# Layer 1's token decays as wide operations, with the weight split moved to ScalarE and VectorE

## The chip, the cores and the metric

The kernel runs on one core of a Trainium2 chip. The metric is the device time of one launch in microseconds (us), the median of repeated runs. A core has five engines that work side by side, each through its own instructions in program order: TensorE (PE in the profile; its weight loads are PEld), VectorE (DVE), ScalarE (ACT), GpSimd (POOL) and SyncE (SP), which here only issues transfers. An engine that waits holds up everything behind it in its own row of instructions. "Sq" behind an engine's name is its queue.

## The reference

One inference step over 128 context and 1024 latent tokens, two layers. Layer 0 mixes with gated linear attention, layer 1 with a gated DeltaNet; each is followed by a gated feed-forward block. The change is in layer 1's preparation, which cut to its core is, per head (8) and direction (2), in chunks:

```
q, k, v = split(silu(dwconv(u @ w_in)))          # width-3 convolution over tokens
qh = l2norm(q) * dk**-0.5 ;  kh = l2norm(k)
g = -exp(a_log) * softplus(a + dt_bias) ;  beta = sigmoid(bt)
b = cumsum(g)                                     # inside a chunk
ld = exp(where(i >= j, b_i - b_j, -inf))
kk  = strict_lower(einsum('id,jd->ij', kh * beta, kh) * ld)
aqk = einsum('id,jd->ij', qh, kh) * ld
t   = inverse(I + kk)
qd = qh * exp(b) ;  kd = kh * exp(b_last - b)
```

A scan over the chunks follows, then the output projection. The kernel works with chunks of 128 tokens (9 of them) and keeps the lengths of q and k apart, to be divided out later.

## The kernel before

**Stage.** `in_proj1` (L1306) multiplies the layer's input (1024 features, 1152 tokens) by 33 weight blocks of 1024x128, in three token chunks of 384. A chunk of a block is 24 matmuls of 384 columns: each f32 product is made of three (L307 to L309), from a rounded high part and a low rest of weight and input. One block makes q, k, v or the gate z of a head; heads get three or four blocks (the last, seven). The product lies in one of seven PSUM tiles ("ps"), and ScalarE copies it out (`evac_raw`, L660, into "rawc"), or applies silu to it for z.

**Weights.** `Weights.fill` (L237) takes a block's weights from "raw" (two buffers, loaded by SyncE) and splits them on GpSimd: L244 makes "whi", L245 "wlo"; four buffers each. A block's split is asked for when the block two before it starts, and the next load is issued right after it.

**Background work.** `mm_block` calls `tick` between its matmuls: generators in the queue `bg` advance by one `yield`, `PACE1` = 4 of them in each chunk, one generator after the other. What a step emits is placed in each engine's row there and then. `conv` (three VectorE steps L1354 to L1358, one for each product copied out) makes q, k and v; then it queues `delta_v` or `delta_a`. A second queue, `side`, holds `solve`, a chain of small VectorE steps (L1564, L1566).

**`delta_a` for one head** (L1445): SyncE broadcasts the cumulated decays b of both directions to all partitions ("bc", one buffer, L1452). After three ticks ScalarE squares q (L1458); TensorE transposes k, ScalarE copies it and squares it, and VectorE sums the squares ("ss"). Then exp(bc) goes into "NA" on ScalarE, and GpSimd multiplies it by q (L1488); SyncE stores it in "pack". For each of 9 chunks and 2 directions, VectorE makes min(bc - b, mask) on 128x128 (L1496), and ScalarE its exponential with a per-token bias (L317, "bc<-bc,lrho"). Three matmuls with a one-column weight add q's squares over the features (L1502); ScalarE copies each row of lengths (L1504) and SyncE stores it in "qqd". Then, one tick each, nine chunks: k^T k and k^T q on TensorE (L1509, L1510), and one VectorE multiply by both decays into "NA" (L1511). Stores to "xd", "Nd" and "pack" close the head.

`delta` (L1806) is the next stage; its `lengths` reads qqd back, transposes it on TensorE and takes 1/length.

Of the kernel before, what the change touches and what calls it, by code (L numbers as in the profile page):

```python
# [37 lines left out]
PACE = 6  # L38
PACE1 = 4
LAGA = 3  # L40
GL, EL, SL, LL, ML, PL = 6, 5, 4, 1, 0, 2
# [178 lines left out]
class Weights:  # L220
# [3 lines left out]
    def __init__(self, K, order):  # L224
# [3 lines left out]
        self.dma = None  # L228

    def load(self, upto):  # L230
        while self.loaded < min(upto, self.n):
            t = self.K.wp.tile([128, 1024], F32, name="raw", tag="raw", bufs=NRAW)
            (self.dma or self.K.nc.sync).dma_start(t, self.K.I["wall"][self.order[self.loaded]])
            self.raw[self.loaded] = t
            self.loaded += 1

    def fill(self, upto):  # L237
        K, nc = self.K, self.K.nc
        while self.next < min(upto, self.n):
            self.load(self.next + 1)  # L240
            raw = self.raw.pop(self.next)
            hi = K.wp.tile([128, 1024], F32R, name="whi", tag="whi", bufs=NB)
            lo = K.wp.tile([128, 1024], F32R, name="wlo", tag="wlo", bufs=NB)
            nc.gpsimd.tensor_scalar(hi, raw, 1.0, 0.0, op0=ALU.mult, op1=ALU.add)  # L244
            nc.gpsimd.tensor_tensor(lo, raw, hi.bitcast(F32), op=ALU.subtract)  # L245
            self.tiles[self.next] = (hi, lo)
            self.next += 1
            self.load(self.next + NRAW - 1)
# [7 lines left out]
class Kern:  # L256
# [1049 lines left out]
    def in_proj1(self, pre, swap):  # L1306
# [43 lines left out]
        def conv(h, part, raw):  # L1350
# [43 lines left out]
    def gates_body(self, p):  # L1394
# [36 lines left out]

        nc.vector.tensor_tensor(self.kdl, ptv, self.b, op=ALU.subtract)
        for d in range(2):
# [11 lines left out]
    def delta_a(self, h, qT, kT, tp):  # L1445
# [16 lines left out]
        ss = tp.tile([128, NT], F32, name="ss", tag="ss", bufs=2)  # L1462
        for n0 in range(0, NT, 3):
# [11 lines left out]
        self.act(kl, ss, AF.Exp, scale=0.5)  # L1475
        for d in range(2):
            c = 8 * d + h
            nc.vector.tensor_tensor(lrho[:, d], self.lbeta[:, :, c], ss, op=ALU.subtract)
            nc.vector.tensor_tensor(rho[:, d], lrho[:, d], self.kdl[:, :, c], op=ALU.add)
        self.act(rho, rho, AF.Exp)  # L1480

        flat = lambda t: t.rearrange("p n i -> p (n i)")
        for d, t in ((0, Nt[1]), (1, At[1])):
            x = flat(t)
            self.act(x, bc[:, d], AF.Exp)
            for a in (0, TC):
                w = TC if a == 0 else TL
                nc.gpsimd.tensor_tensor(x[:, a:a + w], x[:, a:a + w], qT[:, a + (a > 0):a + (a > 0) + w], op=ALU.mult)  # L1488
            nc.sync.dma_start(self.pack[h, d, :, :, 0].rearrange("n p t -> p n t"), t)
        yield  # L1490

        for d in range(2):
            c = 8 * d + h
            for n in range(NT):
                e = bc[:, d, n * 128:n * 128 + 128]
                nc.vector.scalar_tensor_tensor(e, e, self.b[:, n, c:c + 1], self.v("msk_b" if d else "msk_f"), op0=ALU.subtract, op1=ALU.min)  # L1496
                self.act(e, e, AF.Exp, bias=lrho[:, d, n:n + 1])
                if n % 3 == 2:
                    yield
        for i in range(3):  # L1500
            ps = self.ps()
            nc.tensor.matmul(ps[0:1, :CW], self.v("ones")[:, 0:1], At[0][:, 3 * i:3 * i + 3], start=True, stop=True)  # L1502
            qr = tp.tile([1, CW], F32, name="qr", tag="qr", bufs=2)
            nc.scalar.copy(qr, ps[0:1, :CW])  # L1504
            nc.sync.dma_start(self.qqd[h, i:i + 1], qr)
            yield
        for n in range(NT):
# [298 lines left out]
    def delta(self, up):  # L1806
# [4 lines left out]
        with tc.tile_pool(name="dls", bufs=1, reuse_waits="tile") as tp:  # L1811
# [13 lines left out]

            qq = tp.tile([72, 128], F32, name="qq")
            nc.sync.dma_start(qq, self.qqd.rearrange("h i (n t) -> (h i n) t", t=128))

            def lengths():
                ps = self.ps()  # L1830
                nc.tensor.transpose(ps[:, :72], qq, self.v("ident")[:72, :72])
                rq = self.rq.rearrange("p h n -> p (h n)")
                self.act(rq, ps[:, :72], AF.Sqrt, bias=self.eps)
                nc.vector.reciprocal(rq, rq)
                nc.vector.tensor_scalar(rq, rq, 128.0 ** -0.5, None, op0=ALU.mult)

# [4 lines left out]
            for h in range(8):  # L1841
# [44 lines left out]
    def body(self, es, ew):  # L1886
# [3 lines left out]
        with L("u0", side="right") as up:  # L1890
# [81 lines left out]
```

## Time and profile before

| | us |
|---|---|
| median of 3 runs (lowest to highest) | 3569.97 (3560.07 to 3581.61) |
| the profiled execution, its own time | 3563.03 |
| its span, first to last instruction | 3561.0 |
| TensorE busy | 3194.8 (90%) |
| VectorE busy | 2269.7 (64%) |
| GpSimd busy | 1187.6 (33%) |
| ScalarE busy | 1082.2 (30%) |

The mean clock granted to TensorE is 0.94 of full speed. Layer 1's projection fills about 1606 to 2156 us of the span; a feed-forward stage lies ahead of it, the scan (`delta`) behind it. Busy shares are averages over stages with different limits, so the stage has to be looked at by itself. A row "A <- B" names the wait of A for B.

### The profile page before, as it was taken

To read this page: it belongs to the slowest core of one execution; us is meant where nothing else is said; L and a number is where in the kernel's file an instruction comes from. 1 tells how busy PE (TensorE), PEld (TensorE's weight loads), DVE (VectorE), ACT (ScalarE), POOL (GpSimd) and SP (SyncE) were. 2 spreads that over 40 slices of the span, in tenths; PEclk is the share of its full clock that TensorE was granted. 3 is DMA by queue.
4 is the path that set the end of the run, shared out by engine and by line. 5 is a ranking of instruction groups with operands and counts; after the bars stand their busy time and mean duration, and the time that the engine had idled before them with its cause. 6 is when DMAs were issued, how large, how long until landed. Compare 5 with 4: busy or idle time off the path is not lost.

```text
span 3561.0 us, 54650 instructions
## 1 busy us (share of the span) xinstructions
PE 3194.8 (90%) x21774; PEld 2979.9 (84%) x21774; DVE 2269.7 (64%) x3749; ACT 1082.2 (30%) x2282; POOL 1187.6 (33%) x768
## 2 busy tenths in 40 slices
PE   6988898999999999789879997788869999999887
PEld 4877677899999998778778887688859999999886
DVE  4385565656666677665577784755646676676766
ACT  2434213411111111445353433455553111111133
POOL 1221146222222325543223331344533222322455
PEclk9988979999999999889889998999989999999998
DMA  7312443122222112224554648555401111111132
GB/s 257 99 57 78 162 160 132 66 91 99 89 90 89 42 42 84 83 67 137 154 162 134 216 144 244 167 158 163 126 12 42 42 42 42 43 45 39 60 106 95
DMA packets 248877, 370.18 MB, mean 104 GB/s; under 512 B 67647, under 2 KB 185695, under 8 KB 248240
## 3 DMA queue, kind: packets, MB, share of 16 engines
q1 hardware_dynamic: 240612, 349.54, 30.8%
q10 hardware_dynamic: 7340, 14.92, 1.2%
q8 instruction: 173, 2.83, 0.3%
q0 software_dynamic: 672, 2.23, 0.2%
q14 instruction: 80, 0.66, 0.1%
HBM read 284.69 MB, written 81.93 MB: 103 GB/s over the span
## 4 chain that ended last, share of the span: by engine, by line
PE 64%; DVE 18%; ACT 7%; DMA 7%; issue 2%; SPq 1%; POOL 1%; ACTq 0%; DVEq 0%; POOLq 0%
PE ps L307 18%; PE ps L308 17%; PE ps L309 17%; DVE bc L1496 2%; DVE S L522 2%; DVE lns L531 2%; PE psm L428 1%; DVE lnt L581 1%; DVE cv L737 1%; DVE S L593 1%; ACT UH L621 1%; DMA Nl<-Nd 1%; ACT lnt L623 1%; DVE tY L1564 1%; PE ps L836 1%
## 5 line engine op out<-in xcount | busy, mean ns | idle before, releaser
L307 PE MATMUL ps<-UH,whi 128*128 128x384 f32 (+1 forms) x3408 | 1210.7, 355 | 8.8 <-ACT UH L621 5.3
L308 PE MATMUL ps<-UL,whi 128*128 128x384 f32 (+1 forms) x3408 | 1174.1, 345 | 30.7 <-POOL UL L598 23.2
L309 PE MATMUL ps<-UH,wlo 128*128 128x384 f32 (+1 forms) x3408 | 1170.8, 344 | 3.9 <-POOL wlo L245 3.9
L522 DVE SCALAR_TENSOR_TENSOR S<-ps,mod,S 128x384 f32<-128x384 f32 (+1 forms) x1376 | 603.4, 508 | 457.1 <-PE ps L309 456.2
L244 POOL TENSOR_SCALAR whi<-raw 128x1024 fp32r<-128x1024 f32 x262 | 302.9, 1156 | 1685.8 <-PE ps L308 1178.2
L307 PEld LDWEIGHTS ps<-UH,whi 128*128 128x128 f32 x3408 | 660.0, 194 | 64.7 <-issue 46.0
L308 PEld LDWEIGHTS ps<-UL,whi 128*128 128x128 f32 x3408 | 660.0, 194 | 41.3 <-POOL UL L598 26.2
L245 POOL TENSOR_TENSOR wlo<-raw,whi 128x1024 fp32r<-128x1024 f32 x262 | 662.1, 2527 | 21.8
L309 PEld LDWEIGHTS ps<-UH,wlo 128*128 128x128 f32 x3408 | 659.0, 193 | 4.8 <-POOL wlo L245 4.8
L307 PE MATMUL ps<-hh,whi 128*128 128x384 f32 x1056 | 366.5, 347 | 44.3 <-DVE S L522 20.0
L309 PE MATMUL ps<-hh,wlo 128*128 128x384 f32 x1056 | 362.4, 343 | 4.0 <-POOL wlo L245 4.0
L308 PE MATMUL ps<-hl,whi 128*128 128x384 f32 x1056 | 360.8, 342 | 0.4 <-DVE hl L742 0.4
L317 ACT ACTIVATE cv<-cv 128x1153 f32<-128x1153 f32 (+1 forms) x84 | 82.9, 987 | 769.4 <-DVE cv L696 617.0
L307 PEld LDWEIGHTS ps<-hh,whi 128*128 128x128 f32 x1056 | 202.5, 192 | 56.2 <-issue 29.1
L696 DVE SCALAR_TENSOR_TENSOR cv<-raw,vec,cv 128x1153 f32<-128x1153 f32 x136 | 204.6, 1505 | 4.6
L309 PEld LDWEIGHTS ps<-hh,wlo 128*128 128x128 f32 x1056 | 202.7, 192 | 4.6 <-POOL wlo L245 4.6
L308 PEld LDWEIGHTS ps<-hl,whi 128*128 128x128 f32 x1056 | 202.9, 192 | 1.2 <-DVE hl L742 1.2
L660 ACT COPY raw<-ps 128x384 f32<-128x384 f32 (+2 forms) x272 | 95.1, 408 | 346.1 <-PE ps L309 346.0
L525 POOL TENSOR_TENSOR S<-S,gp 128x384 f32<-128x384 f32 x96 | 97.6, 1019 | 141.5 <-ACT gp L520 141.2
L693 DVE TENSOR_SCALAR cv<-raw,vec 128x1153 f32<-128x1153 f32 x68 | 112.9, 1660 | 13.5 <-ACT raw L660 13.5
L737 DVE SCALAR_TENSOR_TENSOR cv<-ps,vec,cv 128x383 f32<-128x383 f32 (+4 forms) x128 | 61.6, 513 | 81.6 <-ACT edge L733 61.8
L1496 DVE SCALAR_TENSOR_TENSOR bc<-bc,bsum,vecd 128x128 f32<-128x128 f32 x144 | 98.7, 755 | 17.0 <-ACT NA L317 16.9
(291 smaller groups left out, 3996.7 us busy)
## 6 DMA issues: line engine op xcount, KB each, us to landing
raw<-wall SPq DMA_DIRECT2D x260, 512.0 KB
qka<-pack SPq DMA_DIRECT2D x144, 192.0 KB
lnt<-wmod SPq DMA_DIRECT2D x48, 512.0 KB
wm<-wmod SPq DMA_DIRECT2D x40, 512.0 KB
pack<-NA SPq DMA_DIRECT2D x32, 576.0 KB
bc<-brow SPq DMA_DIRECT2D x16, 576.0 KB
Nd<-NA SPq DMA_DIRECT2D x16, 576.0 KB
pack<-cv SPq DMA_DIRECT2D x16, 512.0 KB
```

The costliest lines, as they stand in the source:

```text
L244: nc.gpsimd.tensor_scalar(hi, raw, 1.0, 0.0, op0=ALU.mult, op1=ALU.add)
L245: nc.gpsimd.tensor_tensor(lo, raw, hi.bitcast(F32), op=ALU.subtract)
L307: mm(out, wh, uh, start=first, stop=False)
L308: mm(out, wh, ul, start=False, stop=False)
L309: mm(out, wl, uh, start=False, stop=last)
L522: nc.vector.scalar_tensor_tensor(d, ps[:, lo - c * CW:hi - c * CW], g, d, op0=ALU.mult, op1=ALU.add)
L525: nc.gpsimd.tensor_tensor(d, d, t, op=ALU.add)
L660: nc.scalar.copy(raw[:, d:d + hi - lo], ps[:, lo - c * CW:hi - c * CW])
L693: nc.vector.tensor_scalar(t[i], raws[i][:, 0:n], w[:, 0:1], None, op0=ALU.mult)
L696: nc.vector.scalar_tensor_tensor(t[i], raws[i][:, k:n + k], w[:, k:k + 1], t[i], op0=ALU.mult, op1=ALU.add)
L737: nc.vector.scalar_tensor_tensor(t[i][:, a:b], ps[:, a + o:b + o], w[:, k:k + 1], t[i][:, a:b], op0=ALU.mult, op1=ALU.add)
L1496: nc.vector.scalar_tensor_tensor(e, e, self.b[:, n, c:c + 1], self.v("msk_b" if d else "msk_f"), op0=ALU.subtract, op1=ALU.min)
```

## The change

- **Decays wide.** The 144 steps on 128x128 and their exponentials go. For each direction, `between` adds the bias and takes the minimum with the mask in two VectorE operations on 128x1152 (in place on bc), and one ScalarE exponential on 128x1152 follows. The bias now holds log(beta) - b, made once in the gates.
- **q times its decay** (`decayed`) moves from GpSimd to VectorE; direction 0 goes to At[1], direction 1 to Nt[1]. "rho" becomes a product with a precomputed "wend".
- **Lengths.** Nine matmuls with a one-column moving operand put the lengths into columns of one PSUM tile; one copy writes them to "rq". The store, the load and the transposition of qqd go; the square root stands ahead of the scans.
- **Weights.** In blocks 4 to 32 the split is made by ScalarE (whi) and VectorE (wlo), and it is asked for at the second chunk of a block, one block further ahead.
- **Pace.** Five ticks in a chunk instead of four; each of the nine products takes two ticks; two spare ticks ahead of them; the silu of `conv` gets a step of its own.

```diff
-PACE1 = 4
+PACE1 = 5
...
+LAGN = 2
...
+            if self.shared:
+                nc.scalar.copy(hi, raw)
+                nc.vector.tensor_tensor(lo, raw, hi.bitcast(F32), op=ALU.subtract)
+            else:
+                nc.gpsimd.tensor_scalar(hi, raw, 1.0, 0.0, op0=ALU.mult, op1=ALU.add)
+                nc.gpsimd.tensor_tensor(lo, raw, hi.bitcast(F32), op=ALU.subtract)
...
         def evac(b, c, ps):
...
+            if c == 1 and b > 3:
+                self.W.fill(self.wi + NB - 1)
             self.tick(1, st.get("conv", []))
...
             nc.vector.scalar_tensor_tensor(t, raw[:, 2:1155], w[:, 2:3], t, op0=ALU.mult, op1=ALU.add)
+            yield
             self.silu(t, t)
...
+        def decayed(d, t):
+
+            x = flat(t)
+            self.act(x, bc[:, d], AF.Exp)
+            for a in (0, TC):
+                w = TC if a == 0 else TL
+                nc.vector.tensor_tensor(x[:, a:a + w], x[:, a:a + w], qT[:, a + (a > 0):a + (a > 0) + w], op=ALU.mult)
+            nc.sync.dma_start(self.pack[h, d, :, :, 0].rearrange("n p t -> p n t"), t)
+
+        def between(d):
+
+            e = bc[:, d].rearrange("p (n i) -> p n i", i=128)
+            m = self.v("msk_b" if d else "msk_f").unsqueeze(1).to_broadcast([128, NT, 128])
+            nc.vector.tensor_tensor(e, e, lrho[:, d].unsqueeze(2).to_broadcast([128, NT, 128]), op=ALU.add)
+            nc.vector.tensor_tensor(e, e, m, op=ALU.min)
...
-        for d, t in ((0, Nt[1]), (1, At[1])):
-            x = flat(t)
-            self.act(x, bc[:, d], AF.Exp)
-            for a in (0, TC):
-                w = TC if a == 0 else TL
-                nc.gpsimd.tensor_tensor(x[:, a:a + w], x[:, a:a + w], qT[:, a + (a > 0):a + (a > 0) + w], op=ALU.mult)
-            nc.sync.dma_start(self.pack[h, d, :, :, 0].rearrange("n p t -> p n t"), t)
-        yield
-
-        for d in range(2):
-            c = 8 * d + h
-            for n in range(NT):
-                e = bc[:, d, n * 128:n * 128 + 128]
-                nc.vector.scalar_tensor_tensor(e, e, self.b[:, n, c:c + 1], self.v("msk_b" if d else "msk_f"), op0=ALU.subtract, op1=ALU.min)
-                self.act(e, e, AF.Exp, bias=lrho[:, d, n:n + 1])
-                if n % 3 == 2:
-                    yield
-        for i in range(3):
-            ps = self.ps()
-            nc.tensor.matmul(ps[0:1, :CW], self.v("ones")[:, 0:1], At[0][:, 3 * i:3 * i + 3], start=True, stop=True)
-            qr = tp.tile([1, CW], F32, name="qr", tag="qr", bufs=2)
-            nc.scalar.copy(qr, ps[0:1, :CW])
-            nc.sync.dma_start(self.qqd[h, i:i + 1], qr)
+        decayed(0, At[1])
+        yield
+
+        ps = self.ps()
+        for n in range(NT):
+            nc.tensor.matmul(ps[:, n:n + 1], At[0][:, n], self.v("ones")[:, 0:1], start=True, stop=True)
+        nc.scalar.copy(self.rq[:, h], ps[:, :NT])
+        decayed(1, Nt[1])
+        yield
+        between(0)
+        yield
+        between(1)
+        yield
+        self.act(bc[:, 0], bc[:, 0], AF.Exp)
+        yield
+        self.act(bc[:, 1], bc[:, 1], AF.Exp)
+        for _ in range(LAGN):
             yield
         for n in range(NT):
...
+            yield
             yield
...
         with tc.tile_pool(name="in1", bufs=1, reuse_waits="tile") as p:
             first((2,))
+            self.W.shared = True
             for b in range(4, 33):
                 self.blocks([self.w()], b, range(NC), evac)
+            self.W.shared = False
```

VectorE's row from one head's bias sums to its first products, sixth head; tY and Y are steps of `solve`, "cv" of `conv`. Before:

```order
L1479 TENSOR_TENSOR rho<-lrho,kdl 128x9
L1564 TENSOR_TENSOR tY<-X,Y 128x192
L1566 TENSOR_TENSOR Y<-Y,tY 128x8x24
L1564 TENSOR_TENSOR tY<-X,Y 128x175
L1566 TENSOR_TENSOR Y<-Y,tY 128x7x25
L1496 SCALAR_TENSOR_TENSOR bc<-bc,bsum,vecd 128x128 x12
L1564 TENSOR_TENSOR tY<-X,Y 128x156
L1566 TENSOR_TENSOR Y<-Y,tY 128x6x26
L1564 TENSOR_TENSOR tY<-X,Y 128x135
L1566 TENSOR_TENSOR Y<-Y,tY 128x5x27
L1496 SCALAR_TENSOR_TENSOR bc<-bc,bsum,vecd 128x128 x6
```

And now:

```order
L1480 TENSOR_TENSOR NA<-NA,cv 128x128
L1480 TENSOR_TENSOR NA<-NA,cv 128x1024
L1480 TENSOR_TENSOR NA<-NA,cv 128x128
L1480 TENSOR_TENSOR NA<-NA,cv 128x1024
L1589 TENSOR_TENSOR tY<-X,Y 128x220
L1591 TENSOR_TENSOR Y<-Y,tY 128x10x22
L1589 TENSOR_TENSOR tY<-X,Y 128x207
L1591 TENSOR_TENSOR Y<-Y,tY 128x9x23
L1487 TENSOR_TENSOR bc<-bc,lrho 128x1152
L1488 TENSOR_TENSOR bc<-bc,vecd 128x1152
L1487 TENSOR_TENSOR bc<-bc,lrho 128x1152
L1488 TENSOR_TENSOR bc<-bc,vecd 128x1152
```

Eighteen small steps in two groups have become four wide ones, and the product of q with its decay (L1480), which stood on GpSimd, now lies ahead of them.

ScalarE's row at the same place ("rawc" is a product copied out, "cv" the silu of `conv`). Before:

```order
L317 ACTIVATE NA<-bc 128x1152 x2
L660 COPY rawc_12863<-ps 128x384
L317 ACTIVATE bc<-bc,lrho 128x128 x12
L660 COPY rawc_12863<-ps 128x384
L317 ACTIVATE bc<-bc,lrho 128x128 x6
L1504 COPY qr<-ps 1x384 x2
L660 COPY rawc_12864<-ps 128x128
L660 COPY rawc_12864<-ps 128x256
L1504 COPY qr<-ps 1x384
L660 COPY rawc_12864<-ps 128x384
```

And now:

```order
L324 ACTIVATE NA<-bc 128x1152
L1519 COPY rq<-ps 128x9
L324 ACTIVATE NA<-bc 128x1152
L667 COPY rawc_12862<-ps 128x384
L324 ACTIVATE bc<-bc 128x1152 x2
L667 COPY rawc_12863<-ps 128x128
L667 COPY rawc_12863<-ps 128x256
L248 CAST whi<-raw 128x1024
L667 COPY rawc_12863<-ps 128x384 x2
L322 ACT_TABLE_LOAD
L324 ACTIVATE cv<-cv 128x1153
```

The three copies of lengths (qr), which stood behind the exponentials, have become one (rq) that stands between the first two, and the weights' high part (whi) now stands among the copies out of PSUM.

## Rows read from the trace of the kernel before

**Rows 1.** Windows: a feed-forward stretch and layer 1's projection; columns in the first line.

```profile
core 0: us, PE busy (x) PEld busy (x) DVE busy (x) ACT busy (x) POOL busy (x), PEclk, DMA share, GB/s
700.00:1300.00 600.00, 600.00 (x3613) 568.69 (x3612) 387.85 (x634) 79.15 (x172) 155.35 (x90) 1.00 0.24 81
1640.00:2140.00 500.00, 438.78 (x2440) 405.46 (x2440) 360.34 (x576) 209.73 (x433) 161.75 (x101) 0.92 0.50 157
```

**Rows 2.** The chain of waits by line, 1600 to 2240 us (share of that stretch).

```profile
by line: DVE bc L1496 12.1%; PE ps L307 10.5%; PE ps L308 10.2%; PE ps L309 10.2%; DMA bc<-brow 4.1%; DVE tY L1564 3.2%; PE ps L1509 2.9%; issue 2.8%; PE ps L1510 2.4%; ACT bc L317 1.9%; DVE cv L1358 1.9%; DMA kvd<-vt 1.8%; DMA zd<-zt 1.7%;
```

**Rows 3.** Timeline, TensorE, 1984 to 1996: start us, duration us, instruction, [idle before it].

```profile
1983.75 0.38 PE L1509 MATMUL ps<-cv 128*128 128x128 f32 x2
1983.97 0.39 PE L1510 MATMUL ps<-cv 128*128 128x128 f32 x2
1984.12 0.42 PE L307 MATMUL ps<-UH,whi 128*128 128x384 f32 x1
...
1984.90 0.34 PE L308 MATMUL ps<-UL,whi 128*128 128x384 f32 x1
1985.07 0.34 PE L309 MATMUL ps<-UH,wlo 128*128 128x384 f32 x1
1992.66 0.80 PE L1509 MATMUL ps<-cv 128*128 128x128 f32 x2 [7.25 <-ACT rawc L660]
...
1994.00 0.52 PE L308 MATMUL ps<-UL,whi 128*128 128x384 f32 x1
1994.32 0.52 PE L309 MATMUL ps<-UH,wlo 128*128 128x384 f32 x1
```

**Rows 4.** Timeline, all engines, 1979.5 to 1993, the same columns.

```profile
1980.25 1.17 ACT L317 ACTIVATE NA<-bc 128x1152 f32<-128x1152 f32 x1 [5.39 <-DMA bc<-brow]
...
1981.45 10.18 DVE L1496 SCALAR_TENSOR_TENSOR bc<-bc,bsum,vecd 128x128 f32<-128x128 f32 x12 [5.43 <-ACT NA L317]
...
1981.49 4.93 POOL L1488 TENSOR_TENSOR NA<-NA,cv 128x128 f32<-128x128 f32 x4 [29.62 <-ACT NA L317]
```

**Rows 5.** Timeline, VectorE, 1979.5 to 2000.

```profile
1992.81 1.66 DVE L1496 SCALAR_TENSOR_TENSOR bc<-bc,bsum,vecd 128x128 f32<-128x128 f32 x6
...
1996.38 1.89 DVE L1511 TENSOR_TENSOR NA<-ps,bc 128x512 f32<-128x512 f32 x3
```

**Rows 6.** Waits, 1604 to 2180: who waited for whom, total us, times, longest.

```profile
POOL whi L244 <- DMA raw<-wall: 104.9, 12, 22.0
...
PE ps L1509 <- ACT rawc L660: 27.9, 6, 7.2
...
PE ps L1509 <- DVE NA L1511: 22.4, 4, 10.2
...
ACT NA L317 <- DMA bc<-brow: 16.8, 9, 5.4
...
PE ps L1509 <- ACT qr L1504: 6.8, 2, 4.1
```

**Rows 7.** Groups by line, 1604 to 2180: busy us, mean ns | idle before, releaser.

```profile
L1496 DVE SCALAR_TENSOR_TENSOR bc<-bc,bsum,vecd 128x128 f32<-128x128 f32 x144 | 98.7, 755 | 17.0 <-ACT NA L317 16.9
...
L317 ACT ACTIVATE bc<-bc,lrho 128x128 f32<-128x128 f32 x144 | 47.8, 392 | 49.5 <-DVE bc L1496 49.0
...
L1502 PE MATMUL ps<-NA,vecd 128*1 128x384 f32 x48 | 20.6, 512 | 3.1 <-ACT NA L1467 3.1
...
L317 ACT ACTIVATE NA<-bc 128x1152 f32<-128x1152 f32 x16 | 18.3, 1159 | 16.8 <-DMA bc<-brow 16.8
...
L1459 ACT ACTIVATE NA<-cv 128x1024 f32<-128x1024 f32 x8 | 8.4, 1048 | 0.0
```

**Rows 8.** Groups by line and form, VectorE, 640 to 1600.

```profile
L706 DVE TENSOR_TENSOR hl<-cv,hh 128x1024 fp32r<-128x1024 f32 x18 | 22.0, 1225 | 11.2 <-ACT hh L705 11.2
```

**Rows 9.** Timeline, SyncE's queue, 1970 to 2020.

```profile
2017.51 0.64 SPq L233 DMA_DIRECT2D raw<-wall  x1
```

**Rows 10.** Timeline, GpSimd, 2000 to 2030.

```profile
2025.62 1.06 POOL L244 TENSOR_SCALAR whi<-raw 128x1024 fp32r<-128x1024 f32 x1 [13.36 <-DMA raw<-wall]
```

More of the change, by code (lines that the diff above doesn't have):

```diff
@@ L56 @@
 ILAG = 7
+LAGA = 3
 LAGV = 5
+LAGN = 2
 def _pv(v):
@@ L228, in __init__ @@
         self.dma = None
+        self.shared = False
     def load(self, upto):
@@ L243, in fill @@
             lo = K.wp.tile([128, 1024], F32R, name="wlo", tag="wlo", bufs=NB)
-            nc.gpsimd.tensor_scalar(hi, raw, 1.0, 0.0, op0=ALU.mult, op1=ALU.add)
-            nc.gpsimd.tensor_tensor(lo, raw, hi.bitcast(F32), op=ALU.subtract)
+            if self.shared:
[4 more added lines that the diff above has]
+                nc.gpsimd.tensor_tensor(lo, raw, hi.bitcast(F32), op=ALU.subtract)
             self.tiles[self.next] = (hi, lo)
@@ L1430, in gates_body @@
         self.act(self.dec, ptv, AF.Exp)
-        nc.vector.tensor_tensor(self.kdl, ptv, self.b, op=ALU.subtract)
+        nc.vector.tensor_tensor(self.wend, ptv, self.b, op=ALU.subtract)
+        nc.vector.tensor_tensor(self.wend, self.wend, self.lbeta, op=ALU.add)
+        self.act(self.wend, self.wend, AF.Exp)
+        nc.vector.tensor_tensor(self.lbeta, self.lbeta, self.b, op=ALU.subtract)
         for d in range(2):
@@ L1457, in delta_a @@
         Nt, At = ([NA[:, d, i] for d in range(2)] for i in range(2))
+        flat = lambda t: t.rearrange("p n i -> p (n i)")
+        def decayed(d, t):
[10 more added lines that the diff above has]
+            nc.vector.tensor_tensor(e, e, m, op=ALU.min)
         nc.scalar.activation(At[0][:, 0], qT[:, 0:TC], AF.Square)
@@ L1460, in delta_a @@
         yield
-        ss = tp.tile([128, NT], F32, name="ss", tag="ss", bufs=2)
+        ss = tp.tile([128, 2, NT], F32, name="ss", tag="ss", bufs=2)
         for n0 in range(0, NT, 3):
@@ L1467, in delta_a @@
             nc.scalar.activation(Nt[1][:, n0:n0 + 3].rearrange("p n k -> p (n k)"), ps[:, :CW], AF.Square)
-            nc.vector.tensor_reduce(ss[:, n0:n0 + 3], Nt[1][:, n0:n0 + 3], axis=AX.X, op=ALU.add)
+            nc.vector.tensor_reduce(ss[:, 0, n0:n0 + 3], Nt[1][:, n0:n0 + 3], axis=AX.X, op=ALU.add)
             yield
         nc.sync.dma_start(self.kvd[h, 0], Nt[0])
-        self.act(ss, ss, AF.Ln, bias=self.eps)
         kl, rho = self.kl[:, h], self.rho[:, h]
         lrho = tp.tile([128, 2, NT], F32, name="lrho", tag="lrho", bufs=2)
-        self.act(kl, ss, AF.Exp, scale=0.5)
+        self.act(ss[:, 0], ss[:, 0], AF.Ln, bias=self.eps)
@@ L1476, in delta_a @@
+        self.act(kl, ss[:, 0], AF.Exp, scale=0.5)
+        self.act(ss[:, 1], ss[:, 0], AF.Exp, scale=-1.0)
         for d in range(2):
-            c = 8 * d + h
[L1478 to L1482, printed above, removed]
-        for d, t in ((0, Nt[1]), (1, At[1])):
-            x = flat(t)
-            self.act(x, bc[:, d], AF.Exp)
-            for a in (0, TC):
-                w = TC if a == 0 else TL
-                nc.gpsimd.tensor_tensor(x[:, a:a + w], x[:, a:a + w], qT[:, a + (a > 0):a + (a > 0) + w], op=ALU.mult)
-            nc.sync.dma_start(self.pack[h, d, :, :, 0].rearrange("n p t -> p n t"), t)
@@ L1490, in delta_a @@
-        yield
-        for d in range(2):
-            c = 8 * d + h
-            for n in range(NT):
-                e = bc[:, d, n * 128:n * 128 + 128]
-                nc.vector.scalar_tensor_tensor(e, e, self.b[:, n, c:c + 1], self.v("msk_b" if d else "msk_f"), op0=ALU.subtract, op1=ALU.min)
-                self.act(e, e, AF.Exp, bias=lrho[:, d, n:n + 1])
-                if n % 3 == 2:
-                    yield
-        for i in range(3):
-            ps = self.ps()
-            nc.tensor.matmul(ps[0:1, :CW], self.v("ones")[:, 0:1], At[0][:, 3 * i:3 * i + 3], start=True, stop=True)
-            qr = tp.tile([1, CW], F32, name="qr", tag="qr", bufs=2)
-            nc.scalar.copy(qr, ps[0:1, :CW])
-            nc.sync.dma_start(self.qqd[h, i:i + 1], qr)
+            nc.vector.tensor_tensor(lrho[:, d], self.lbeta[:, :, 8 * d + h], ss[:, 0], op=ALU.subtract)
@@ new lines, in delta_a @@
+            nc.vector.tensor_tensor(rho[:, d], ss[:, 1], self.wend[:, :, 8 * d + h], op=ALU.mult)
+        yield
+        decayed(0, At[1])
[11 more added lines that the diff above has]
+        self.act(bc[:, 0], bc[:, 0], AF.Exp)
@@ L1823, in delta @@
             self.drain([self.inverse(Q[0]["N"], Q[0]["U"], Q[0]["T"], tp)])
[L1826 to L1835, printed above, removed]
+            rq = self.rq.rearrange("p h n -> p (h n)")
+            self.act(rq, rq, AF.Sqrt, bias=self.eps)
+            nc.vector.reciprocal(rq, rq)
+            nc.vector.tensor_scalar(rq, rq, 128.0 ** -0.5, None, op0=ALU.mult)
             def done(h):
@@ L1871, in delta @@
                     nc.sync.dma_start(Q[h]["z"], self.zd[h])
-                if h == 0:
-                    lengths()
                 if h == 3:
@@ L1936, in body @@
             self.load_vec("vecd", p)
-            self.lbeta, self.b, self.kdl = (p.tile([128, NT, 16], F32, name=x) for x in ("lbeta", "bsum", "kdl"))
+            self.lbeta, self.b, self.wend = (p.tile([128, NT, 16], F32, name=x) for x in ("lbeta", "bsum", "wend"))
             self.kl = p.tile([128, 8, NT], F32, name="kl")
```

2 lines of the change are left out of this document (removed).

## The prediction, made before the change was run

> **What bounds the kernel now.** I read the windows first, to see how the stage of the change differs from one that runs well [rows 1]. From 700 to 1300 us TensorE has no gap and a granted clock of 1.00. From 1640 to 2140, in layer 1's projection, it is busy for 438.8 of 500 us, so 61 us are gaps, and the clock is 0.92. The clock has two levels (1.2 and 2.4 GHz), so 0.92 means that 16% of the stretch, 80 us, ran at the low one; work done there takes twice as long, and about 40 us are lost. VectorE is busy for 360 us, ScalarE for 210: neither is full. The stage is TensorE's, less about 100 us that it loses by waiting.
>
> The chain of waits says on whom: the largest single entry, ahead of any matmul line, is VectorE's L1496 with 12.1% [rows 2]. The timeline of TensorE shows one such wait [rows 3]: the matmuls start 0.17 us apart (1984.90, 1985.07), then comes a gap of 7.25 us, until ScalarE has copied a product out of PSUM, and after the gap they start 0.32 us apart, at the low clock. The gap and the clock are one loss with two parts.
>
> Why ScalarE was late stands in the timeline of all engines [rows 4]. The broadcast bc came 5.39 us after ScalarE was ready for it. Then GpSimd multiplied q by its decay for 4.93 us, and in that time and during the weight split behind it twelve steps of L1496 took 10.18 us. A few microseconds later six of them took 1.66 us, 0.277 us each [rows 5]: the steps are short, but not beside GpSimd. ScalarE's exponentials alternate with them, and its copies out of PSUM stand behind those exponentials, so TensorE runs out of its seven PSUM tiles. The first product of the head (L1511) is made at 1996.38, 16.1 us after bc landed. Twelve waits of this kind, on ScalarE's rawc and qr and on VectorE's NA, sum to 27.9 + 22.4 + 6.8 = 57 us [rows 6]; they are nearly all of the 61.
>
> **The change part by part.** The sum is made against the profiled execution, 3563.0 us; the median of the runs is 7 us above it.
>
> VectorE's load. The 144 small steps go: 98.7 us as they stand [rows 7], but only 144 x 0.277 = 40 us if nothing stood beside them; 59 us are contention. In their place come 32 operations on 128x1152. The nearest is the 128x1024 subtraction of the feed-forward, 1.225 us [rows 8], which is itself partly run beside GpSimd; by width that gives 1.38 us, 44 us in all. The product with q comes over from GpSimd: 16 times a 128x1024 (1.2) and a 128x128 (0.25), 23 us. The weights' low part is exactly the operation of rows 8: 29 x 1.2 = 35 us. So VectorE's busy time moves by -99 + 44 + 23 + 35 = +3 us: it stays at about 360 us, 70 to 75% of a shorter stage. The gain isn't in its load, but in where it falls: no burst of 18 steps beside GpSimd, which keeps only the small copies and memsets of `solve`.
>
> ScalarE. 144 exponentials of 0.39 us make room for 16 of 1.16 [rows 7], -38 us; the high part of the weights costs 29 x 1.05 (the 128x1024 square of L1459), +30 us. It stays under half busy.
>
> The chain that TensorE waits for. After bc lands: exponential 1.2, product with q 1.4 for each direction (the second exponential runs beside the first product), four small steps of `solve` 1.5, four wide operations 5.5, the last exponential 1.2: 12.2 us to the first L1511, against 16.1. And three PSUM tiles are no longer held: before, the three copies of lengths stood in ScalarE's row behind all 18 exponentials; now one copy stands ahead of the wide ones. With 2.5 products in a chunk instead of 4, a chunk uses 3.5 PSUM tiles in some 4.9 us (24 matmuls of 0.173 and what lies between them), so three tiles are about 4 us of patience. Against that, TensorE gets to the first product sooner: seven ticks at five a chunk behind the exponential, where it was nine at four, some 4 us. What each head gains by the shorter chain and by the tiles, 8 us, is half eaten by this.
>
> What is late next: the broadcast. It is issued behind the stores of the head before, and ScalarE waited for it nine times, 16.8 us in all, 5.4 at most [rows 6]. The change makes none of these transfers smaller, and a TensorE that waits less gets to that place earlier. I let three or four heads keep a wait of 5 us, and the others 1 us: 22 us of gaps are left of the 61, and clock losses in proportion, 14 of 40. Saved: 39 + 26 = 65 us. Bounds: nothing, if bc stays the end of the chain in every head, and 101, if all waits go.
>
> The lengths. 24 matmuls of 384 columns go, 20.6 us of records [rows 7], on the path wherever TensorE is the end. 72 with one moving column come, but each needs 128 columns of weights. The trace has no such operation. Two matmuls of 128 moving columns with a weight load each take 0.37 us before the next can start (1983.75 to 1984.12) [rows 3], 0.18 each; a single one costs at least nothing and at most the whole pair, 0.37. That is 13 us by the middle value, which I take since it is the nearest row: -7 us net, between -21 and +6. The Trainium skill's "TensorE: Matmul & The Clock Gate", section "LDWEIGHTS (loading the stationary operand)", speaks against this edit: a load costs its columns over 1.2 in ns, whatever the moving side has. By it 144 loads (two passes per matmul, as the 48 records of L1502 for 24 matmuls show) are an estimated 15 us, and the edit would bring 5 us, not 7. No run before has a one-column moving operand.
>
> The new wait. GpSimd waited 12 times for a raw weight, 104.9 us, at most 22.0 [rows 6], and nobody minded, since it runs ahead. Now ScalarE and VectorE wait for it, and behind ScalarE's copy stand the copies out of PSUM. A load issued at 2017.51 [rows 9] was there for GpSimd at 2025.62 [rows 10]: 8 us. In the new order a load is issued when the block before it is split, one block ahead, and a block is at least 72 x 0.173 = 12.5 us of TensorE. That covers 8 us; it doesn't when SyncE is late itself behind a head's stores. I charge 12 us for it and for other queueing in the two rows (below: 0, since seven PSUM tiles hide a wait of a few us; above: the 105 us).
>
> The rest. The readback of the lengths and its transposition leave `delta`; they were a few operations among waits for transfers: nothing. More ticks per chunk and the extra step in `conv` move work by less than a chunk: nothing, unless the stage's end gets a tail.
>
> Sum: 3563.0 - 65 - 7 + 12 = 3503, and 7 more for the median: 3510 us.
>
> **The rivals.** *The broadcast holds.* The chain of stores, load and broadcast of a head is as long as before, TensorE merely gets to it sooner. For it: the waits for bc, and 4.1% of the stage's chain in that transfer [rows 2]. Against it: L1496 has three times that share. Gaps 45, clock 30, lengths -7, new waits 8: -61 + 45 - 40 + 30 - 7 + 8 = -25, 3545 us.
>
> *All waits go.* The pace of one product in two ticks is slow enough for VectorE everywhere: -61 - 40 - 7 and 5 for new waits: -103, 3467 us. Against it: bc's lateness isn't touched.
>
> *Slower: the raw weights stop ScalarE.* If GpSimd's 12 waits fall on ScalarE's row in full, 105 us, and PSUM hides some 4 us of each, 57 us of gaps are new, and by today's ratio of clock to gap (40 to 61) another 37. With 72 saved that is +22: 3592 us. It decides from the point at which a load lands over 4 us behind ScalarE's reaching the copy, in about every third block. For it: the loads stand in SyncE's row among stores that themselves wait for VectorE, which now waits for the loads. Against it: the loads are asked for earlier than before. The same page of the Trainium skill (section "Architectural detail: the array is 16× 32×32, not 1× 128×128") calls the rows of ScalarE and VectorE strictly first in, first out; nothing then gets past such a copy, as the exponentials in rows 4 already show.
>
> *It doesn't do what it says.* If L1496 is slow for another reason than GpSimd, the wide operations would be slow too. The same instruction at 0.277 and at 0.85 us within 12 us speaks against this; its time would be that of the first rival.
>
> **Chances.** The forecast 0.55 (its own range 3485 to 3532), the broadcast holds 0.20, all waits go 0.15, slower 0.10. The range for eight in ten, 3462 to 3562, takes in the first two rivals and leaves the slower one out. What runs of this kernel can tell from no change is about 0.5%, 18 us, so faster means less than 3552 us. That is the forecast, all waits gone and about half of the first rival: 0.81; within 0.5%: 0.10; slower: 0.09.
>
> **What would show it.** Right: in the projection the granted clock rises to 0.96 or more, TensorE's gaps fall to some 20 us, those left stand behind bc or raw; the wide operations take 1.3 to 1.4 us each; the stage is 50 to 70 us shorter, and the stages around it as long as before. The lengths: 72 matmuls in less than 20 us. Wrong: waits of ScalarE for raw of over 40 us in sum, gaps of over 40 us behind it or behind VectorE's wide steps, or wide steps of 2 us and more. A gain that lies outside the stage would be another cause than mine.

## The result, and the profile after

The changed kernel takes 3529.44 us (median of 4 runs, 3509.85 to 3550.28) against 3575.79 for the kernel before (4 runs): a ratio of 0.9886, interval 0.9852 to 0.9919, faster by some 46 us. The forecast was 3510, 60 us below the median of 3 runs known then (3570), with 3462 to 3562 as its range.

To compare profiles I cut out layer 1's projection by its own first and last work, the first copy into `abs` and the last silu into `zt`, and call that the stage. It is a better measure than the whole: the identical code ahead of the stage ended between 1584.9 and 1609.2 us in the 14 profiles of this study, so one run of the whole says little about 20 us, while the stage came out at 531.4 and 528.9 us in two profiles of the changed kernel. The windows of the stage, of the kernel before (columns as in rows 1; the last two lines are a gap and what follows it):

```profile
1588.20:2162.90 574.70, 511.46 (x2844) 475.91 (x2842) 381.42 (x608) 245.41 (x495) 174.77 (x113) 0.93 0.50 159
...
1985.40:1992.60 7.20, 0.01 (x1) 0.00 (x0) 7.10 (x13) 3.31 (x10) 4.43 (x3) 0.84 0.70 217
1992.60:1995.00 2.40, 2.34 (x9) 2.34 (x10) 2.40 (x8) 1.82 (x8) 0.00 (x0) 0.50 0.00 0
```

and of the changed kernel: the two stretches of [rows 1], the stage, and the largest gap that is left with what follows it.

```profile
700.00:1300.00 600.00, 600.00 (x3617) 568.03 (x3616) 386.78 (x628) 80.32 (x175) 155.62 (x90) 1.00 0.23 80
1640.00:2140.00 500.00, 464.00 (x2810) 452.95 (x2810) 336.64 (x553) 204.79 (x336) 17.00 (x19) 0.94 0.55 175
...
1597.50:2128.90 531.40, 499.79 (x2936) 487.00 (x2934) 340.66 (x554) 228.06 (x376) 16.30 (x18) 0.96 0.54 171
...
1973.30:1979.30 6.00, 0.00 (x0) 0.00 (x0) 5.86 (x8) 2.80 (x5) 0.00 (x0) 0.68 0.35 110
1979.30:1982.20 2.90, 2.89 (x10) 2.89 (x11) 2.87 (x6) 1.28 (x2) 0.00 (x0) 0.50 0.00 0
```

The stage is 43.3 us shorter. TensorE's gaps (span less busy) went from 63.2 to 31.6 us; its busy time fell by 11.7. VectorE is busy 40.8 us less, though it took over two kinds of work from GpSimd. The groups by line of the changed kernel, for [rows 7]:

```profile
L249 DVE TENSOR_TENSOR wlo<-raw,whi 128x1024 fp32r<-128x1024 f32 x32 | 39.2, 1224 | 48.5 <-ACT whi L248 43.9 <-issue 4.4
L1366 DVE SCALAR_TENSOR_TENSOR cv<-rawc,vec,cv 128x1153 f32<-128x1153 f32 x24 | 34.4, 1434 | 0.2
...
L1480 DVE TENSOR_TENSOR NA<-NA,cv 128x128 f32<-128x128 f32 (+1 forms) x32 | 22.5, 755 | 15.9 <-ACT NA L324 12.4 <-ACT rq L1519 3.4
L1488 DVE TENSOR_TENSOR bc<-bc,vecd 128x1152 f32<-128x1152 f32 x16 | 21.7, 1358 | 0.6
L1487 DVE TENSOR_TENSOR bc<-bc,lrho 128x1152 f32<-128x1152 f32 x16 | 21.6, 1351 | 0.0
```

And its waits, for [rows 6]:

```profile
ACT bc L324 <- DVE bc L1488: 47.2, 15, 6.6
ACT whi L248 <- DMA raw<-wall: 25.0, 7, 5.0
ACT NA L324 <- DMA bc<-brow: 10.6, 8, 2.9
PE ps L1518 <- ACT NA L1490: 8.1, 2, 5.2
PE ps L1533 <- ACT rawc L667: 6.4, 2, 6.0
PE ps L1533 <- DVE NA L1535: 6.0, 5, 2.7
PE ps L843 <- ACT cv L324: 3.8, 2, 3.2
PE ps L314 <- ACT whi L248: 1.5, 1, 1.5
```

The 57 us that TensorE waited for rawc, qr and NA have become 12.4 (6.4 + 6.0). A new one stands at the lengths, 8.1 us: they now run early, straight behind ScalarE's squares of q (L1490), which wait for the stores of the head before. The largest gap left is the old kind in a new form; here it is in the changed kernel's timeline of all engines:

```profile
1964.90 1.17 ACT L324 ACTIVATE NA<-bc 128x1152 f32<-128x1152 f32 x1 [2.91 <-DMA bc<-brow]
...
1968.08 1.17 ACT L324 ACTIVATE NA<-bc 128x1152 f32<-128x1152 f32 x1 [1.97 <-DMA bc<-brow]
...
1972.16 1.35 DVE L1487 TENSOR_TENSOR bc<-bc,lrho 128x1152 f32<-128x1152 f32 x1
1973.55 1.36 DVE L1488 TENSOR_TENSOR bc<-bc,vecd 128x1152 f32<-128x1152 f32 x1
...
1975.00 1.16 ACT L324 ACTIVATE bc<-bc 128x1152 f32<-128x1152 f32 x1 [5.38 <-DVE bc L1488]
...
1977.66 1.16 ACT L324 ACTIVATE bc<-bc 128x1152 f32<-128x1152 f32 x1 [1.50 <-DVE bc L1488]
1978.73 0.52 ACT L667 COPY rawc<-ps 128x128 f32<-128x128 f32 x2
...
1979.31 0.79 PE L1533 MATMUL ps<-cv 128*128 128x128 f32 x2 [6.02 <-ACT rawc L667]
...
1979.63 1.88 DVE L1535 TENSOR_TENSOR NA<-ps,bc 128x512 f32<-128x512 f32 x3
```

ScalarE's two exponentials stand in its row until VectorE's wide steps are done, and the copy that TensorE needs stands behind them.

### The profile page after: what moved, and what is told of

Read it like the earlier page. It is cut to its first block, busy times and chain, and to the rows that moved or that the text cites. A ratio compares the mean times of both kernels' runs of the same rounds, so it can differ in the third digit from the quotient of the medians.

```text
span 3532.0 us, 54392 instructions
## 1 busy us (share of the span) xinstructions
PE 3197.8 (91%) x21869; PEld 2999.5 (85%) x21869; DVE 2231.6 (63%) x3703; ACT 1065.1 (30%) x2165; POOL 1027.7 (29%) x672
## 5 line engine op out<-in xcount | busy, mean ns | idle before, releaser
L251 POOL TENSOR_SCALAR whi<-raw 128x1024 fp32r<-128x1024 f32 x230 | 263.6, 1146 | 1520.2 <-PE ps L315 1087.7
L252 POOL TENSOR_TENSOR wlo<-raw,whi 128x1024 fp32r<-128x1024 f32 x230 | 580.1, 2522 | 19.2
L1593 POOL COPY X<-Y 128x1024 f32<-128x1024 f32 (+1 forms) x5 | 10.2, 2036 | 482.8 <-DVE Y L1591 425.6
```

## The experiments

The stage of every kernel, from one windows row each; gaps are span less busy, and "at low clock" is how much of the busy time fell into stretches with a granted clock of 0.50, summed over them. The ratios are to the kernel before, run beside each group on its chip.

| kernel | median us, ratio (interval) | stage | TensorE busy | gaps | at low clock |
|---|---|---|---|---|---|
| before | 3575.79 | 574.7 | 511.5 | 63.2 | 55.0 |
| after | 3529.44, 0.9886 (0.9852 to 0.9919) | 531.4 | 499.8 | 31.6 | 41.4 |
| e4 free GpSimd | 3556.42, 0.9921 (0.9889 to 0.9953) | 556.5 | 505.8 | 50.7 | 43.6 |
| e5 and lengths | 3546.97, 0.9915 (0.9886 to 0.9945) | 542.0 | 501.8 | 40.2 | 47.8 |
| e6 and wide form | 3542.66, 0.9919 (0.9886 to 0.9953) | 543.4 | 501.9 | 41.5 | 36.8 |
| e13 all three | 3531.43, 0.9864 (0.9828 to 0.99) | 531.6 | 492.8 | 38.8 | 31.5 |
| e7 and new split place | 3528.1, 0.9844 (0.9789 to 0.99) | 520.0 | 494.8 | 25.2 | 35.1 |
| e12 = e7 again | 3521.62, 0.9849 (0.9802 to 0.9896) | 518.4 | 493.2 | 25.2 | 32.5 |
| e11 = after again | 3531.03, 0.9883 (0.9841 to 0.9924) | 528.9 | 495.7 | 33.3 | 33.6 |
| e1 lengths late | 3543.05, 0.991 (0.988 to 0.994) | 542.6 | 495.5 | 47.1 | 34.1 |
| e2 split on GpSimd | 3550.63, 0.9923 (0.9895 to 0.9951) | 541.4 | 500.0 | 41.4 | 47.8 |
| e3 decay on GpSimd | 3543.69, 0.9915 (0.9892 to 0.9938) | 535.2 | 498.2 | 37.0 | 38.2 |
| e8 more lag | 3539.92, 0.9874 (0.9827 to 0.9921) | 527.4 | 494.5 | 32.9 | 33.4 |
| e9 own squares, old pace | 3519.02, 0.9848 (0.9811 to 0.9885) | 516.8 | 492.0 | 24.8 | 27.8 |

**e4: the kernel before with GpSimd freed, and nothing else.**

```diff
+            self.W.shared = True    # split on ScalarE and VectorE, blocks 4 to 32
-                nc.gpsimd.tensor_tensor(x[:, a:a + w], x[:, a:a + w], qT[...], op=ALU.mult)
+                nc.vector.tensor_tensor(x[:, a:a + w], x[:, a:a + w], qT[...], op=ALU.mult)
```

> The kernel before, with only the engines changed: the split of blocks 4 to 32 on ScalarE and VectorE, at its old place, and the product of q and its decay on VectorE. The 144 small steps, their exponentials, the lengths and the pace are those of before. Theory A (contention): the small steps fall from 0.69 us each to 0.3, and the stage falls by 20 to 35 us, to 540 to 555. Rival B (the form: 18 steps and 18 exponentials in turn are the trouble): the stage stays above 565 although the steps are short.

Stage 556.5, 18.2 us shorter, a little less than the 20 to 35 I expected. VectorE's groups of e4, then the burst in its timeline that answers to the twelve steps of [rows 4]:

```profile
L1504 DVE SCALAR_TENSOR_TENSOR bc<-bc,bsum,vecd 128x128 f32<-128x128 f32 x144 | 41.0, 358 | 0.0
```

```profile
1982.54 3.24 DVE L1504 SCALAR_TENSOR_TENSOR bc<-bc,bsum,vecd 128x128 f32<-128x128 f32 x12
```

The same instruction, the same head: 10.18 us for twelve beside GpSimd, 3.24 without it; 144 of them 98.7 us and 41.0, the 40 that the prediction worked out. That the steps were slow because of GpSimd is shown. The Trainium skill's "SBUF — State Buffer", section "Who interferes with whom", states that a VectorE instruction with two inputs in SBUF contends with GpSimd's reads; these rows agree. But the 58 us freed on VectorE brought 18 on the stage: TensorE still waited 22.2 us for rawc and 13.1 for qr.

**e3 and e2: the changed kernel with one of the two back on GpSimd.**

```diff
-                nc.vector.tensor_tensor(x[:, a:a + w], ...)   # e3: q x decay
+                nc.gpsimd.tensor_tensor(x[:, a:a + w], ...)
-            self.W.shared = True                              # e2: weight split
```

> The changed kernel, with the product of q and its decay back on GpSimd; all else as changed. Theory A (contention): these 4.9 us a head lie just ahead of the wide steps and beside them; the wide steps rise by 1 to 2 us each where they meet, and they can't start earlier; the stage rises by 8 to 15 us, to about 543. Rival B (the form): VectorE is relieved of 22.5 us, and the stage stays within 4 us of 531.

> The changed kernel, with the weights' split back on GpSimd everywhere (at its new, earlier place). Theory A (contention: VectorE is slow beside GpSimd, and freeing GpSimd brings most of the gain): VectorE's wide steps (L1487, L1488, 1.35 us now) rise to 2 us or more in the mean, the stage loses 15 to 25 of the 43 us, to 546 to 556. Rival B (the wide form brings the gain; GpSimd's share is small, and ScalarE and VectorE are relieved of 33 and 39 us): the stage stays at 527 to 536. In both, ScalarE's 25 us of waits for raw weights go.

The stage grew by 3.8 and 10.0 us (6.3 and 12.5 against e11, the changed kernel run again). Neither is what I expected of contention: e3 was to cost 8 to 15 us and is nearer to its rival, and e2, with 15 to 25 expected, lies between the two. The groups of e3:

```profile
L1480 POOL TENSOR_TENSOR NA<-NA,cv 128x128 f32<-128x128 f32 (+1 forms) x32 | 65.3, 2069 | 358.8 <-ACT rq L1519 222.2 <-ACT NA L324 87.8 <-DMA bc<-brow 48.8
...
L1487 DVE TENSOR_TENSOR bc<-bc,lrho 128x1152 f32<-128x1152 f32 x16 | 31.2, 1950 | 6.3 <-ACT NA L324 4.9 <-ACT rq L1519 1.4
L1488 DVE TENSOR_TENSOR bc<-bc,vecd 128x1152 f32<-128x1152 f32 x16 | 26.4, 1649 | 0.6
```

and of e2:

```profile
L252 POOL TENSOR_TENSOR wlo<-raw,whi 128x1024 fp32r<-128x1024 f32 x32 | 85.4, 2668 | 2.7
L1588 DVE TENSOR_TENSOR tY<-X,Y 128x31 f32<-128x31 f32 (+15 forms) x94 | 51.3, 546 | 18.2 <-DMA X<-xd 16.6
...
L1487 DVE TENSOR_TENSOR bc<-bc,vecd 128x1152 f32<-128x1152 f32 x16 | 21.7, 1358 | 0.6
```

In e3 both engines pay. The product runs with the wide steps, which go from 1.35 to 1.95 and 1.65 us, though little of that reaches the stage. In e2 the split misses them (1358 ns, as in the changed kernel, where I had expected 2 us and more) and hits `solve`'s products instead (546 ns for 339).

**e5, e6 and e13: the lengths, the wide form, and both, on a freed GpSimd.** All three keep the old pace and the split at a block's start.

```diff
+                    nc.tensor.matmul(ps[:, n:n + 1], At[0][:, n], self.v("ones")[:, 0:1], ...)   # e5, e13, ahead of the exponentials
-            nc.tensor.matmul(ps[0:1, :CW], self.v("ones")[:, 0:1], At[0][:, 3 * i:3 * i + 3], ...)
+        between(0)   # e6, e13: 32 wide steps instead of 144 small ones
+        between(1)
```

> GpSimd freed and the decays still in 144 small steps, as in e4 (stage 556.5 us, TensorE's gaps about 51, 22.2 us of them at ScalarE's rawc and 13.1 at its qr copies), plus the one-column lengths alone. Theory: of what the change brings beyond a free GpSimd (25 us of stage) a good part is the lengths: some 5 us of TensorE (20.6 us of records become about 16) and the three qr copies that stood behind all exponentials; the waits at qr go, those at rawc fall to some 12 us, the stage comes to about 538. Rival: only the matmuls' own 5 us are won and the wait moves on to the first product's tile: stage 550 to 552, rawc waits still about 20 and waits of the first product for VectorE new.

> The wide decays on a freed GpSimd, with the old lengths (24 matmuls of 384 columns and three copies behind the exponentials), the old pace and the old place of the weight split. Theory: the small steps without GpSimd took 41 us in 144 pieces of 0.285, the wide ones take 43 us in 32: the form itself brings no VectorE time, only 38 us less of ScalarE, so the stage stays within 6 us of e4's 556.5 and the qr and rawc waits stay at 25 us and more. Rival: the wide form is the main part beyond the free GpSimd; the stage falls to about 540 and rawc plus qr to under 15 us.

> The wide decays and the one-column lengths together, at the old pace, with the weight split where it was (at a block's start) and without the extra step in conv: e7 less those two edits, or e5 and e6 put together. Free GpSimd alone has a stage of 556.5 us, with the lengths 542.0 (-14.5), with the wide form 543.4 (-13.1), with both and the two edits 520.0 and 518.4. Theory: lengths and wide form add up (the one frees tiles, the other shortens the chain), so this comes to 529 us, and the last 10 us are the split's new place: in the middle of a block it meets no copy that TensorE waits for, while at a block's start TensorE waits for whi. Waits of the first products for rawc 10 us and more. Rival: the new place brings nothing, the lengths and the form help each other, 517 to 523, rawc waits under 6 us.

The lengths bring 14.5 us, the wide form 13.1, both 24.9 (531.6): they nearly add up, and with the 18.2 of e4 they are as much as the whole change. For e6 I had taken the form to be worth under 6 us, since it spares VectorE nothing (43.3 us for 41.0); the rival's 540 was nearer. The two remove different waits. Those of e5:

```profile
PE ps L1516 <- ACT rawc L666: 11.7, 6, 3.0
PE ps L1500 <- ACT NA L1465: 9.6, 2, 9.1
```

and of e6:

```profile
PE ps L314 <- ACT qr L1529: 23.0, 6, 6.1
PE ps L1534 <- ACT rawc L667: 5.2, 3, 3.1
```

In e4 rawc stood at 22.2 us and qr at 13.1. The lengths take qr away and halve rawc; the form takes most of rawc, and qr grows to 23.0, because its copies still stand behind the exponentials.

**e1: the changed kernel with the lengths behind the exponentials.**

```diff
-        ps = self.ps()   # 9 lengths and their copy, ahead of decayed(1)
+        ps = self.ps()   # the same, just ahead of the first product
```

> The changed kernel, with the nine one-column matmuls and their copy moved from between the two products with q to just ahead of the first k^T k. The stage is measured from the first copy of abs to the last silu into zt: 574.7 us before, 531.4 in the changed kernel. Theory A (TensorE now stands directly behind ScalarE's square of q, which waits for the last head's stores; 9 us of gaps at L1518, about 6 us of low clock behind them): the waits at the lengths go and the stage falls by 10 to 15 us, to about 518. Rival (the wait only moves on to the products or to ScalarE's copies): the gaps come back at L1533, the stage stays within 4 us of 531.

The wait at the squares is gone, but against theory A the stage is 11.2 us longer: TensorE waits 13.1 us for NA, 9.9 for rawc and 5.1 for the lengths' copy. So the early place pays, and its 8.1 us wait is the cheaper one; that it pays by the PSUM tile that isn't held is my reading.

**e7, e11 and e12: the pace.** The change gives five ticks a chunk and two per product.

```diff
-PACE1 = 5
+PACE1 = 4
-            yield   # the second of two behind each product
```

> The changed kernel with four ticks a chunk and one tick per product again, so products come denser. Theory: VectorE's product (0.44 us each here) keeps up with one every 1.3 us, so the pace is worth under 4 us: stage 528 to 536, waits of the first products for VectorE's NA stay under 10 us. Rival: products in a denser row queue up in PSUM: waits for NA 15 us and more, stage 540 or more.

> The changed kernel once more, with nothing edited, beside the next run and the one before it on the same chip. It tells how far a stage repeats: theory, within 4 us of 531.4, and the old pace is then 8 us and more faster; rival: the stage varies by 10 us from one execution to another, and the 11 us between it and e7 say nothing.

> The changed kernel at the old pace (four ticks a chunk, one tick per product) once more, in the same session as the changed kernel itself. Theory: stage 518 to 523, and a median 8 to 12 us below the changed kernel's, since the products of a head are done earlier, its stores go out earlier, and the next head finds its buffers free. Rival: no difference between the two, stage 525 to 531.

Against my expectation for e7 the new pace costs about 11 us of stage (531.4 and 528.9 with it, 520.0 and 518.4 without). The medians of the pair run together are 9 us apart, which their intervals don't separate; the stages do. The waits of e11 (its lines are one higher):

```profile
ACT bc L325 <- DVE bc L1489: 47.1, 15, 6.6
...
PE ps L1534 <- ACT rawc L668: 9.9, 2, 6.7
```

and of e12:

```profile
ACT bc L324 <- DVE bc L1488: 23.5, 14, 3.8
...
PE ps L314 <- ACT rawc L667: 4.1, 1, 4.1
...
PE ps L1533 <- ACT rawc L667: 1.7, 2, 1.0
```

With the new pace the exponentials stand in ScalarE's row twice as long behind VectorE, with the copies out of PSUM behind them. That this is what costs the 11 us is argued, not shown: TensorE's waits for rawc fall from 9.9 us to 5.8 (4.1 + 1.7) in this pair, but only from 6.4 to 6.0 between the changed kernel and e7; the rest is spread over cv, `abT` and NA. The reason that I gave for e12, that a head's stores go out earlier and free the next head's buffers, does not show: ScalarE's squares wait 25.6 us for stores in e12 and 24.4 in the changed kernel. Which of the pace's two halves does it was not tried. And e7 less e13 is the split's new place with the extra step in `conv`: 12 us, by rawc waits of 14.8 us (12.7 + 2.1) that fall to 6.0. Those two edits were not taken apart either; my reason for e13, that TensorE waits for whi at a block's start, is not it (3.9 us there, 3.3 in e7).

**e8 and e9: the gaps that are left.**

```diff
-LAGA = 3                                        # e8, on the changed kernel; LAGV 5 to 7
+LAGA = 5
-        nc.scalar.activation(At[0][:, 0], ...)  # e9, on e7: squares in v's tile
+        sq = tp.tile([128, NT, 128], F32, name="sq", tag="tv")
+        nc.scalar.activation(sq[:, 0], ...)
```

> The changed kernel with two more ticks between a head's steps ahead of its lengths (LAGA 5 for 3, LAGV 7 for 5). Of the 31.6 us of gaps left, 8.1 us stand at the lengths behind ScalarE's square of q (which waits for the stores of the head before) and 4.1 us at the transposes of ab, 3.8 at cv. Theory: these waits are a matter of when TensorE gets there, and 0.4 of a chunk, some 2 us, later they lose about half: stage 526 to 530, gaps about 27. Rival: work moved later falls on the next chunk and on the next head's stores: the gaps stay at 30 us or more and the stage at 531 to 540.

> The changed kernel at the old pace (as e7, stage 520.0 us), and the squares of q in a tile of their own buffer (the one that v's transposes use, another 128x1152) instead of a quarter of NA, so that they needn't wait for the stores of the head before. In e7 the lengths wait 9.3 us for these squares, 7.5 of them in one gap at 1722.69. Theory: the wait is the buffer's; it goes, with some 3 us of clock behind it: stage 508 to 512, gaps about 16 us. Rival: the next writer of NA, ScalarE's copy of the transposed k, waits for the same stores and ScalarE's copies out of PSUM stand behind it: the gap moves to rawc or to the transposes' tile, stage 517 to 523.

e8 is inconclusive: 527.4 against 528.9 and 531.4, gaps as before, and the lengths wait 9.8 us. In e9 the rival held, near enough: 516.8, 1.6 to 3.2 us shorter than e12 and e7. (The edit also gives a buffer of layer 0, outside the stage, another tag.) ScalarE's timeline of e7,

```profile
1729.80 0.31 ACT L1490 ACTIVATE NA<-cv 128x128 f32<-128x128 f32 x1 [14.34 <-DMA pack<-NA]
```

and of e9:

```profile
1709.03 0.31 ACT L1491 ACTIVATE sq<-cv 128x128 f32<-128x128 f32 x1
...
1724.15 0.48 ACT L1499 COPY NA<-ps 128x384 f32<-128x384 f32 x1 [13.87 <-PE ps L316]
```

The squares are early, and ScalarE stands still just as long at the next writer of NA, until the same moment (132.5 us into the stage in e7, 133.1 in e9). The releaser named in e9 is an instruction of TensorE; that it is the stores again is my reading of the equal moments. e9 has the lowest median, 3519.02, and with e12 beats both kernels by the stage; by the medians it is not told apart from the changed kernel.

## Why the prediction was right, and where it missed

The mechanism held in its parts. VectorE's small steps were slow beside GpSimd (e4); the wide operations take 1.35 us, 43.3 in all (44 predicted); the product with q 22.5 (23); the split's low part 39.2 (35, which counted 29 blocks where 32 were split so). The gain lies in the stage: the 477.5 us from its end to the first copy into `hh` of the next feed-forward are 479.5 in the changed kernel and 485.5 in e11, so nothing is gained there. But the stage lost 43 us where the sum had 60. Of the signs I had set, the time of the wide steps and that of the 72 matmuls (19.1 us) came true; the stage was to be 50 to 70 us shorter, and the gaps some 20 us, behind bc or raw.

- *Gaps, 61 to 22.* They fell to 31.6. What I said would be late next was not: the broadcast costs ScalarE 10.6 us, 2.9 at most, and TensorE nothing by name. Left instead are the lengths behind the head's stores (8.1 us, a wait that I didn't see although I moved it), the exponentials behind VectorE, and `abT` and `cv`. Of the pace and the extra step in `conv` I wrote "nothing"; the pace cost about 11 us, and the split's new place with the extra step, without a price in the sum too, brought about 12. That the two cancel is luck: e13, without either, has the stage of the changed kernel (531.6). From bc to the first product that head took 14.7 us (1964.90 to 1979.63), not 12.2: the second half of bc came 2.0 us late, and behind the last exponential the sum left out the copy out of PSUM and the matmuls, 0.8 us.
- *The clock, 40 to 14.* This term failed most. "80 us, ran at the low one" and "about 40 us are lost" counted the gaps in: the granted clock is already 0.84 in the 7.2 us gap and 0.68 in the 6.0 us gap above, and a low clock costs nothing while TensorE stands. The sums over all stretches of the stage with a granted clock of 0.50, for the kernel before, the changed kernel and e11:

```profile
sum 81.92, PE 54.97 PEld 50.27 DVE 65.69 ACT 60.37 POOL 15.16; mean PE 5.00 PEld 4.57 DVE 5.97 ACT 5.49 POOL 1.38
...
sum 47.81, PE 41.40 PEld 41.13 DVE 33.37 ACT 33.19 POOL 1.12; mean PE 5.17 PEld 5.14 DVE 4.17 ACT 4.15 POOL 0.14
...
sum 40.96, PE 33.61 PEld 32.91 DVE 29.41 ACT 26.05 POOL 1.13; mean PE 6.72 PEld 6.58 DVE 5.88 ACT 5.21 POOL 0.23
```

  Before the change TensorE stood for 27 of those 81.9 us and worked for 55. Half of the work is the price (matmuls 0.32 us apart instead of 0.17): an estimated 27 us, not 40. It fell to 21 us, in e11 to 17, so the change gave back 7 to 11 us, not 26. Two profiles of the same kernel, with nearly equal gaps (31.6 and 33.3), differ by 4 us, so what the price goes by these runs don't settle.
- *The lengths, -7.* Their own matmuls took as long as before. TensorE's timeline, of the kernel before,

```profile
1849.78 0.81 PE L1502 MATMUL ps<-NA,vecd 128*1 128x384 f32 x2
1850.51 0.44 PE L307 MATMUL ps<-UH,whi 128*128 128x384 f32 x1
```

  and of the changed one:

```profile
1727.65 3.57 PE L1518 MATMUL ps<-vecd,NA 128*128 128x1 f32 x16 [0.36 <-ACT NA L1491]
...
1908.84 2.06 PE L1518 MATMUL ps<-vecd,NA 128*128 128x1 f32 x18
1910.76 0.42 PE L314 MATMUL ps<-UH,whi 128*128 128x384 f32 x1
```

  Start to start a matmul of 384 columns took 0.73 us, not the 0.86 that 20.6 us of overlapping records made of it; all 24 took 18.9. The 18 loads of a head took 1.92 us, 0.107 each, which is the figure of the Trainium skill's "TensorE: Matmul & The Clock Gate", section "LDWEIGHTS (loading the stationary operand)", 128 columns over 1.2: the trace agrees. But in the two heads that wait for the squares they run behind a gap, at half the clock (3.57 us for 16), and all 144 took 19.1. At one clock the edit did bring something: busy time less half of what fell at the low clock is 484.0 us before, 484.0 in e4 and 483.5 in e6, all with the old lengths, and 479.1 in the changed kernel, 478.9 in e11, 477.9 in e5 and 477.1 in e13, with the new ones. That is an estimated 5 to 7 us, so the term was about right; where the part beyond the lengths' own matmuls lies is not shown. Of the 14.5 us of e5, 10.5 are gaps and 4.0 busy time, so most of it is not matmul time. I take it to be the PSUM tiles, which I had put into a balance that comes to little; this is by elimination.
- *Raw weights, +12.* ScalarE waited 25.0 us for them, 5.0 at most, TensorE 2.1 behind the split (1.5 for whi, 0.6 for wlo). So the slower rival, by which these waits stop ScalarE, fell; so did the one in which the broadcast holds, and the one in which the steps are slow for another reason than GpSimd (e4).
- *VectorE's load, +3.* It fell by 41. I had freed only the 144 steps; `conv` and `solve` met GpSimd too (conv's last step 1736 to 1434 ns, L1358 then and L1366 now). ScalarE's exponentials between tokens went from 47.8 to 18.7 us, 29 less and not 38, since their records overlap; the sum doesn't use it.

So the stage gave 43 us and not 60. By the changed kernel's own profile the gaps were set 7 us too high, the clock 19 and the lengths 2, some 28 us; against that the 12 us charged for the raw weights fell away, since what they cost lies in the gaps above. That the total lay in the range owes something to these offsets. I had put VectorE's gain down to "no burst of 18 steps beside GpSimd"; freeing GpSimd alone is 18 of the 43 us, and the lengths and the wide form bring the other 25 (e13).

## What to carry to other kernels

Read an operation's time alone and beside its neighbours before counting what it costs; here the two differed threefold, and other operations that met the neighbour gained as well when it was moved, though the 58 us saved on the small steps were worth 18 to the stage. When TensorE waits for PSUM, look at what stands ahead of the copy in its engine's row: an instruction put there before its input is ready holds up everything behind it. Try each part of a change by itself: two parts here cancelled. Price a lowered clock by the work done at the low level, not by the time spent there.

## What the runs showed of the hardware

A 6.0 us gap was followed by 2.9 us at 1.2 GHz (granted clock 0.50), a 7.2 us gap by at least 2.4 us. In e3 the meeting cost both engines: GpSimd's product took 65.3 us for 32, against 39.8 in the kernel before, where it met the small steps, and VectorE's wide steps 57.6 us (31.2 + 26.4) against 43.3.
